# Norm of the last feed-forward sub-layer by tiles of 128 tokens, with its first blocks in two halves of tokens

## Chip, cores and metric

The kernel runs on one core of a Trainium2 chip. The metric is the device time of one execution in microseconds (us), the median of several runs. Engines are named as in the profile: PE (matrix products and transposes), PEld (its weight loads, which overlap products), DVE (vector engine), ACT (activation engine), POOL, and SP, which here issues the DMA loads of the weights.

## What is computed

Two layers of a trunk over 256 latent tokens and 256 context tokens of 1024 channels. Each layer runs a feed-forward sub-layer, a token-mixing block and another feed-forward sub-layer; the last one of the second layer runs for the latent tokens alone. The part that matters here is the end of the last mixing block and the start of the sub-layer behind it:

```
def modulated_norm(xs, gain, mod, s):
    return rms_norm(xs, gain) * (1.0 + mod_vec(mod, 3 * s + 1)) + mod_vec(mod, 3 * s)

def gated_residual(xs, y, gain, mod, s, weight):
    return xs + weight * mod_vec(mod, 3 * s + 2) * rms_norm(y, gain)

xl = gated_residual(xl, yl, norm_post[l, 1], mod_l, 1, 1.0)      # yl: output of the mixing block
a, g = jnp.split(modulated_norm(xl, g_pre, mod, 2) @ w_in_f, 2)  # 1024 -> 2 x 2816
xl = gated_residual(xl, (jax.nn.silu(a) * g) @ w_out_f, g_post, mod, 2, 0.5)
```

## The kernel before

Tokens lie in tiles of 128 (one partition each): two latent tiles, 0 and 1, and two context tiles. A product of float32 matrices is made of three matmuls (`mm3`, lines 285 to 287), with both operands split into a rounded high part and the rest (`hi`, `lo`). The weights come by DMA into two raw buffers (`wraw`), and `Ring.ahead` splits them on ACT (`whi`, L208) and DVE (`wlo`, L211) into three pairs of buffers, a number of pieces ahead of their use. Each engine takes its instructions in the order in which the program issues them, since the schedule is written out by hand; `tick` moves a clock of the program that paces side tasks and these splits.

`natural_out` ends a sub-layer: it computes the output by token tiles with 512 channels at a time (half `h` = 0, then 1). For two tiles, and in the last half, it runs all products of tile 0, then those of tile 1. After each tile come `first` (sum of squares on ACT, `z` on DVE, L501) and `update` (reciprocal root in `rstd`, and the residual stream `x` in two halves, L512), with the squares of the new `x` for the next norm (`PreNorm.square`, L400 on ACT). In tile 1's products stands `K.W.ahead(0)`, which splits the first weights of the sub-layer behind.

When both tiles are updated, the next norm runs for both together: `stats` (L425 and `rstd`, on two columns), `scale` (`xs`, L433, four instructions), `transpose` (16 transposes on PE, L292, into PSUM banks that hold the two tiles' columns side by side), and `modulate` (ACT writes `h`, L459, 256 tokens wide, DVE splits it into `hThi`, L462, and `hTlo`, L463).

`ffn` then takes 44 blocks of 128 output channels: 11 groups `c`, each with two blocks for `a` (part 0) and two for `g` (part 1). A block is 8 x 3 matmuls with the weights as the stationary operand of 128 x 128 and the tokens as the moving operand, `N` columns: 512 in the sub-layers with context, 256 in the last one. `evacuate` takes a block out of PSUM (silu on ACT, L649, product on DVE, L653, split on both). In the sub-layers with context (`nt == 4`) the first three blocks run on the latent half (256 columns) first; `ctx_norm` stands in the middle of the third one, and then the three second halves follow. In the last sub-layer (`nt == 2`) there is no such split: every block takes its 256 columns at once.

Of the kernel before, what the change touches and what calls it, by code (L numbers as in the profile page):

```python
# [14 lines left out]
P = 128  # L15
# [240 lines left out]
def tick(K, us):  # L256

    K.clock += us
    for t in list(K.tasks):
        if t.done:  # L260
            K.tasks.remove(t)
        elif t.wake <= K.clock:
            t.step(K.clock)
# [26 lines left out]
def transpose(K, out, x):  # L290
    n = x.shape[0]
    K.nc.tensor.transpose(out, x, K.ident[:n, :n])  # L292
# [10 lines left out]
def t2k(K, name="t2k"):  # L303
    return K.tp.tile([P, 512], F32, tag="t2k", name=name)
# [98 lines left out]
class PreNorm:  # L403
# [25 lines left out]
    def scale(self, st, h):  # L429
        K = self.K  # L430
        for t in range(2):
# [2 lines left out]
                                      scalar2=None, op0=OP.mult)  # L434
            self.xs[h, t] = xs

    def transpose(self, st, h, bank=aux_tile):
        K = self.K
        pts = [bank(K) for _ in range(2)]
        for b in range(4):  # L440
            for t in range(2):
                o = 256 * (b % 2) + P * t
                transpose(K, pts[b // 2][:, o:o + P], self.xs[h, t][:, P * b:P * b + P])
        self.pts[h] = pts
# [21 lines left out]
def natural_out(K, y1, lhi, llo, nk, wview, tiles, G, nxt, hold, free):  # L466
# [55 lines left out]
    for h in range(2):  # L522
        pss = {t: mm_tile(K) for t in tiles}
        nh = len(hold) if h == 1 and hold and len(tiles) > 2 else min(3 + h * len(hold), n)
        for i in range(n - nh):
            s = piece(i, h, None if h == 1 and hold else min(K.W.nsub - 1, n - 1 - i))
            for t in tiles:
                part(pss[t], s, t)
        if h == 0:
            subs = [piece(i, h, n - 1 - i) for i in range(n - nh, n)]  # L530
            for t in tiles:
                for j, s in enumerate(subs):
                    part(pss[t], s, t)
                    if t == tiles[-1]:
                        K.W.ahead(j)
                square_sum(K, pss[t], ss[:, t, 0:1])
                v.tensor_tensor(out=y1[:, t, :], in0=pss[t], in1=G[:, t // 2, 0:512], op=OP.mult)
            nc.scalar.activation(warm, K.ident[:, 0:1], AF.Sqrt)
            continue
        if nxt is not None:  # L540
            pn = nxt()
        if len(tiles) == 2:
            subs = [piece(i, h, min(K.W.nsub - 1, n - 1 - len(hold) - i)) for i in range(n - nh, n)]
            for t in tiles:
                for j, s in enumerate(subs):
                    part(pss[t], s, t)
                    if t == 1 and pn is not None and j == 1:
                        K.W.ahead(0)
                first(t)
                update([t])  # L550
            if pn is not None:
                pn.stats(0)
                for q in range(2):
                    pn.scale(0, q)
                    pn.transpose(0, q)
                K.W.ahead(1)
                for q in range(2):
                    pn.modulate(0, q)
        else:
            subs = []  # L560
            for i in range(n - nh, n):
                subs.append(piece(i, h, min(K.W.nsub - 1, n - 1 - i)))
                part(pss[0], subs[-1], 0)
            first(0)
            update([0])
            K.W.ahead(1)
            for s in subs:
                part(pss[1], s, 1)
            first(1)
            update([1])  # L570
            pn.stats(0)
            pn.scale(0, 0)
            pn.scale(0, 1)
            for s in subs:
                part(pss[2], s, 2)
            first(2)
            for i, s in enumerate(subs):
                part(pss[3], s, 3)
                if i < 2:
                    pn.transpose(0, i)  # L580
                    pn.modulate(0, i)
                if i == 0:
                    update([2])
            first(3)
            update([3])
            K.W.ahead(K.W.nsub - 1)
            pn.stats(1)
# [29 lines left out]
def ffn(K, l, s, f, pn, tiles, nxt, jobs, every=(5.0, 7.6), pools=None, prep=False):  # L617
# [8 lines left out]
    with pools.es as es:  # L626
# [5 lines left out]
        def mm_block(ps, sub, c0, c1, half_way=None):  # L632
            whi, wlo = sub
            for b in range(8):
                if b == 4 and half_way is not None:
                    half_way()
                mm3(K, ps[:, c0:c1], whi[:, b, :], wlo[:, b, :], hi[:, b, c0:c1], lo[:, b, c0:c1], b == 0, b == 7)
                if (b == 3 and c1 - c0 == 512) or b == 7:
                    tick(K, 2.6)

        early = []
        n_early = 3 if nt == 4 else 0
        sas = []
        blocks = [(c, part, n) for c in range(11) for part in range(2) for n in range(2)]

# [12 lines left out]
        for i, (c, part, n) in enumerate(blocks):  # L658
# [11 lines left out]
            if i >= n_early:  # L670
                mm_block(ps, sub, 0, N)
                evacuate(c, part, n, ps)
                continue
            mm_block(ps, sub, 0, 256, (lambda: ctx_norm(K, pn)) if i == n_early - 1 else None)
            early.append((ps, sub))
            if i == n_early - 1:
                for j, (ps, sub) in enumerate(early):
                    mm_block(ps, sub, 256, 512)
                    K.W.ahead(j)
                    evacuate(*blocks[j], ps)  # L680
        finish(K, ada)
# [1111 lines left out]
```

## Time and profile before

| | us |
|---|---|
| median of 3 runs (2197.65 to 2198.15) | 2197.89 |
| the profiled execution | 2197.24 |
| its span, first to last instruction | 2195.2 |

| engine | busy us | share of the span |
|---|---|---|
| PE | 2116.6 | 96% |
| PEld | 1710.9 | 78% |
| DVE | 1116.4 | 51% |
| ACT | 769.3 | 35% |

Times in the rows are us from the span's start, and those of a single instruction in the group views ns. A busy PE is not PE at its peak, since matmuls overlap each other by their latency: the distance from one start to the next tells the rate. The change lies between 1983 and 2010 us; the last sub-layer's first 44 blocks end at 2127.6 and the rest is its output.

### The profile page before, as it was taken

How to read it: one execution, taken by the hardware profiler on the slowest of the kernel's cores; microseconds unless marked ns; L12 is line 12 of the kernel's file. 1: busy time of each engine (PE TensorE's matmuls, PEld its weight loads, DVE VectorE, ACT ScalarE, POOL GpSimd, SP SyncE). 2: the span in 40 equal slices, each digit the busy share in tenths (PEclk: the TensorE clock that was granted, in tenths of full speed). 3: DMA queues.
4: the chain of work that ended last, by engine and by line, in shares of the span. 5: the costliest groups of instructions: out<-in, count | busy, mean ns of one | idle time of the engine just before them, and what ended most of it. 6: DMA issues, size and time to landing. Idle time of an engine off the chain costs nothing.

```text
span 2195.2 us, 28897 instructions
## 1 busy us (share of the span) xinstructions
PE 2116.6 (96%) x11691; PEld 1710.9 (78%) x11691; DVE 1116.4 (51%) x2038; ACT 769.3 (35%) x1282; POOL 315.9 (14%) x288
## 2 busy tenths in 40 slices
PE   6999999999999999999999999999999989998998
PEld 4766778888867778777777877778888878888997
DVE  4895332357544655633332258733324685756554
ACT  4213222343543333422222233322223345355443
POOL 0242000002323300000000024400000144440000
PEclk9999999999999999999999999999999999999999
DMA  9457542344312223355554335643223454444554
GB/s 312 172 206 257 185 146 91 115 139 135 109 62 87 76 79 112 121 176 189 182 183 164 106 117 187 225 148 115 92 82 127 171 168 128 128 140 139 188 186 145
DMA packets 211613, 323.11 MB, mean 147 GB/s; under 512 B 13176, under 2 KB 154104, under 8 KB 211480
## 3 DMA queue, kind: packets, MB, share of 16 engines
q1 hardware_dynamic: 196864, 287.17, 38.4%
q0 software_dynamic: 8560, 27.63, 3.9%
q10 hardware_dynamic: 6056, 6.46, 1.0%
q8 instruction: 92, 1.51, 0.3%
q14 instruction: 41, 0.34, 0.0%
HBM read 307.57 MB, written 14.71 MB: 147 GB/s over the span
## 4 chain that ended last, share of the span: by engine, by line
PE 82%; DVE 9%; issue 3%; ACT 3%; DMA 2%; POOL 1%; ACTq 0%; DVEq 0%; SPq 0%; POOLq 0%
PE mm L285 25%; PE mm L286 24%; PE mm L287 24%; PE aux L341 3%; PE aux L292 2%; DVE wlo L211 1%; DVE hTlo L463 1%; PE aux L1434 1%; DMA wraw<-in_w_ffn_in_dram 1%; ACT jk L400 1%; ACT whi L208 1%; PE aux L1559 1%; DVE hThi L462 1%; DVE at_mx L1408 1%; PE aux L1157 1%
## 5 line engine op out<-in xcount | busy, mean ns | idle before, releaser
L285 PE MATMUL mm<-hThi,whi 128*128 128x512 f32 (+1 forms) x1992 | 716.1, 360 | 10.4 <-DVE hThi L462 5.5
L287 PE MATMUL mm<-hThi,wlo 128*128 128x512 f32 (+1 forms) x1992 | 699.6, 351 | 7.3 <-DVE wlo L211 4.0
L286 PE MATMUL mm<-hTlo,whi 128*128 128x512 f32 (+1 forms) x1992 | 699.9, 351 | 1.5 <-DVE hTlo L463 0.7
L211 DVE TENSOR_TENSOR wlo<-wraw,whi 128x1024 fp32r<-128x1024 f32 (+1 forms) x295 | 362.5, 1234 | 429.6 <-ACT whi L208 428.1
L285 PEld LDWEIGHTS mm<-hThi,whi 128*128 128x128 f32 x1992 | 379.3, 190 | 120.4 <-issue 49.6
L208 ACT ACTIVATE whi<-wraw 128x1024 fp32r<-128x1024 f32 (+1 forms) x351 | 367.1, 1049 | 235.0 <-PE mm L287 173.7
L287 PEld LDWEIGHTS mm<-hThi,wlo 128*128 128x128 f32 x1992 | 379.3, 190 | 59.5 <-DVE wlo L211 5.4
L286 PEld LDWEIGHTS mm<-hTlo,whi 128*128 128x128 f32 x1992 | 379.5, 191 | 50.2 <-DVE hTlo L463 4.0
L211 POOL TENSOR_TENSOR wlo<-wraw,whi 128x1024 fp32r<-128x1024 f32 x56 | 138.0, 2471 | 239.9 <-ACT whi L208 223.1
L653 DVE TENSOR_TENSOR sa<-sa,mm 128x512 f32<-128x512 f32 (+1 forms) x88 | 54.3, 617 | 145.4 <-PE mm L287 145.4
L649 ACT ACTIVATE sa<-mm 128x512 f32<-128x512 f32 (+1 forms) x88 | 47.7, 543 | 216.1 <-PE mm L287 214.3
L286 PE MATMUL mm<-wlo,ha 128*128 128x512 f32 x308 | 120.0, 389 | 0.0
L285 PE MATMUL mm<-whi,ha 128*128 128x512 f32 x308 | 120.0, 389 | 0.0
L287 PE MATMUL mm<-whi,ha 128*128 128x512 f32 x308 | 119.8, 389 | 0.0
L655 ACT ACTIVATE ha<-sa 128x512 fp32r<-128x512 f32 (+1 forms) x44 | 25.4, 578 | 244.0 <-DVE sa L653 244.0
L655 ACT ACTIVATE hb<-sa 128x512 fp32r<-128x512 f32 (+1 forms) x44 | 25.5, 579 | 178.3 <-DVE sa L653 169.8
L285 PE MATMUL mm<-whi,hThi 128*128 128x512 f32 (+2 forms) x224 | 81.9, 366 | 5.1 <-ACT whi L208 5.1
L286 PE MATMUL mm<-wlo,hThi 128*128 128x512 f32 (+2 forms) x224 | 80.5, 359 | 2.4 <-DVE wlo L211 2.4
L388 POOL DMA_DIRECT2D gd<-ev x12 | 6.8, 574 | 513.9 <-ACT whi L208 356.7
L287 PE MATMUL mm<-whi,hTlo 128*128 128x512 f32 (+2 forms) x224 | 79.5, 355 | 0.0
L285 PE MATMUL mm<-whi,hb 128*128 128x512 f32 x188 | 73.1, 389 | 0.0
L286 PE MATMUL mm<-wlo,hb 128*128 128x512 f32 x188 | 73.1, 389 | 0.0
(441 smaller groups left out, 2859.5 us busy)
## 6 DMA issues: line engine op xcount, KB each, us to landing
wraw<-in_w_ffn_in_dram SPq DMA_DIRECT2D x88, 1024.0 KB
wraw<-in_w_in_dram SPq DMA_DIRECT2D x42, 1024.0 KB
wraw<-in_w_ffn_out_dram SPq DMA_DIRECT2D x40, 1024.0 KB
adaG<-in_w_ada_dram SPq DMA_DIRECT2D x33, 1024.0 KB
aday<-in_w_ada_dram SPq DMA_DIRECT2D x33, 1024.0 KB
wraw<-in_w_out_dram SPq DMA_DIRECT2D x7, 1024.0 KB
ha<-in_w_ada_dram SPq DMA_DIRECT2D x6, 1024.0 KB
r_tq<-tab SPq DMA_DIRECT2D x8, 768.0 KB
```

The costliest lines, as they stand in the source:

```text
L208: K.nc.scalar.activation(h3, r, AF.Copy)
L211: (self.eng or K.lo_eng).tensor_tensor(out=l3, in0=r, in1=h3.bitcast(F32), op=OP.subtract)
L285: mm(out, ahi, bhi, start=first, stop=False)
L286: mm(out, ahi, blo, start=False, stop=False)
L287: mm(out, alo, bhi, start=False, stop=last)
L292: K.nc.tensor.transpose(out, x, K.ident[:n, :n])
L341: nc.tensor.matmul(ps[o:o + 32, :], self.K.sc[:, k + i, :], w[:, i, 512 * b:512 * b + 512], start=k == 0, stop=k == 6, tile_position=(0, o))
L400: K.nc.scalar.activation(jk[:, :src.shape[-1]], src, AF.Square, scale=1.0 / 32.0, accum_out=acc)
L462: nc.vector.tensor_copy(oh, hv)
L649: nc.scalar.activation(sa[:, :N], ps[:, :N], AF.Silu)
L653: nc.vector.tensor_tensor(out=g[:, :N], in0=g[:, :N], in1=ps[:, :N], op=OP.mult)
L655: nc.scalar.activation(hh, g[:, :N], AF.Copy)
```

## The change

It replaces the norm of both tiles by two norms of one tile each, in the last mixing block only (the one place where `natural_out` has two tiles and a norm behind it). `tile_scale(t)` runs directly behind `update([t])`, inside the loop over tiles: sum, reciprocal root and the scaling of that tile's two halves. `tile_out(t, dve)` makes 8 transposes into two PSUM banks (one for each half of the channels) and modulates one tile: of four blocks of 128 x 128, three on ACT and the one in `dve` on DVE, and DVE splits 512 elements into the tile's columns of `hThi` and `hTlo`. Tile 0's `tile_out` stands behind the loop, tile 1's in the middle of the third block's first half. The last sub-layer's first three blocks get the two halves that the others have, here of 128 columns, and `tick` counts a half of 128 columns as 1.3 in place of 2.6. The number of pieces that are split ahead in these three blocks becomes 2, 1 and 0 instead of 2 each, and the splits stand behind the second halves.

```diff
+    def tile_scale(self, t):
+        K = self.K
+        rs = K.sm.tile([P, 2], F32, tag="pn_rs", name="pn_rs", bufs=2)[:, 0:1]
+        rst = K.sm.tile([P, 2], F32, tag="pn_rst", name="pn_rst", bufs=2)[:, 0:1]
+        ss = self.ss[0]
+        K.nc.vector.scalar_tensor_tensor(out=rs, in0=ss[:, t:t + 1, 0], scalar=RMS_EPS, in1=ss[:, t:t + 1, 1], op0=OP.add, op1=OP.add)
+        rstd(K, rst, rs, 1)
+        for h in range(2):
+            xs = t2k(K, "xs")
+            K.nc.vector.tensor_scalar(out=xs, in0=K.x[:, t, 512 * h:512 * h + 512], scalar1=rst, scalar2=None, op0=OP.mult)
+            self.xs[h, t] = xs
+
+    def tile_out(self, t, dve):
+        K, nc, v = self.K, self.K.nc, self.K.nc.vector
+        A, B = K.AB[self.l, self.s]
+        pts = [aux_tile(K) for _ in range(2)]
+        for h in range(2):
+            for b in range(4):
+                transpose(K, pts[h][:, P * b:P * b + P], self.xs[h, t][:, P * b:P * b + P])
+        for h in range(2):
+            h32 = t2k(K, "h32")
+            for b in range(4):
+                o, p = h32[:, P * b:P * b + P], pts[h][:, P * b:P * b + P]
+                a, c = A[:, 4 * h + b, 0:1], B[:, 4 * h + b, 0:1]
+                if b in dve:
+                    v.tensor_scalar(out=o, in0=p, scalar1=a, scalar2=c, op0=OP.mult, op1=OP.add)
+                else:
+                    nc.scalar.activation(o, p, AF.Identity, scale=a, bias=c)
+            hv = h32.rearrange("p (k c) -> p k c", k=4)
+            oh = self.hi[:, 4 * h:4 * h + 4, P * t:P * t + P]
+            v.tensor_copy(oh, hv)
+            v.tensor_tensor(out=self.lo[:, 4 * h:4 * h + 4, P * t:P * t + P], in0=hv, in1=oh.bitcast(F32), op=OP.subtract)
...
                 first(t)
                 update([t])
+                if pn is not None:
+                    pn.tile_scale(t)
             if pn is not None:
-                pn.stats(0)
-                for q in range(2):
-                    pn.scale(0, q)
-                    pn.transpose(0, q)
+                pn.tile_out(0, (3,))
                 K.W.ahead(1)
-                for q in range(2):
-                    pn.modulate(0, q)
...
-                    tick(K, 2.6)
+                    tick(K, min(2.6, (c1 - c0) / 98.0))
...
-        n_early = 3 if nt == 4 else 0
+        n_early = 3
...
-            mm_block(ps, sub, 0, 256, (lambda: ctx_norm(K, pn)) if i == n_early - 1 else None)
+            mm_block(ps, sub, 0, N // 2, (lambda: ctx_norm(K, pn) if nt == 4 else pn.tile_out(1, (3,))) if i == n_early - 1 else None)
...
-                    mm_block(ps, sub, 256, 512)
+                    mm_block(ps, sub, N // 2, N)
```

## Rows read from the trace of the kernel before

**Rows 1.** The page's first part: each engine's busy time, share and instructions

```profile
PE 2116.6 (96%) x11691; PEld 1710.9 (78%) x11691; DVE 1116.4 (51%) x2038; ACT 769.3 (35%) x1282; POOL 315.9 (14%) x288
```

**Rows 2.** Stretches: length, busy us of PE, PEld, DVE, ACT, POOL, PEclk, DMA share, GB/s

```profile
1988.70:1996.25 7.55, 0.00 (x0) 0.00 (x1) 5.30 (x16) 3.83 (x10) 1.05 (x2) 0.65 0.11 30
1996.25:1999.76 3.51, 3.51 (x16) 3.30 (x17) 3.35 (x7) 2.17 (x5) 0.00 (x0) 0.50 0.77 241
1999.76:2003.70 3.94, 3.85 (x26) 3.65 (x25) 3.84 (x8) 3.81 (x6) 0.00 (x0) 0.82 0.80 266
2003.70:2009.50 5.80, 5.80 (x50) 5.80 (x49) 2.87 (x3) 2.66 (x4) 0.00 (x0) 1.00 0.31 98
2009.50:2127.60 118.10, 118.10 (x987) 118.10 (x986) 65.88 (x82) 54.32 (x81) 0.00 (x0) 1.00 0.55 183
```

**Rows 3.** Waits of PE from 1983 to 2010: who waited for whom, us, times, longest

```profile
PE aux L292 <- DVE xs L433: 7.6, 1, 7.6
```

**Rows 4.** DVE's timeline around the norm: start, us, instruction, idle before and releaser

```profile
1985.88 0.75 DVE L512 SCALAR_TENSOR_TENSOR x<-z,po_rst,x 128x512 f32<-128x512 f32 x1
...
1989.19 1.23 DVE L211 TENSOR_TENSOR wlo<-wraw,whi 128x1024 fp32r<-128x1024 f32 x1 [1.89 <-ACT whi L208]
1990.33 0.68 DVE L501 TENSOR_TENSOR z<-mm,G 128x512 f32<-128x512 f32 x1
...
1992.14 0.75 DVE L512 SCALAR_TENSOR_TENSOR x<-z,po_rst,x 128x512 f32<-128x512 f32 x1
...
1994.49 0.16 DVE L425 SCALAR_TENSOR_TENSOR pn_rs<-pn_ss 128x2 f32<-128x2 f32 x1 [0.94 <-ACT jk L400]
...
1995.71 1.68 DVE L433 TENSOR_SCALAR xs<-x,pn_rst 128x512 f32<-128x512 f32 x4
...
1998.64 0.43 DVE L462 CAST hThi<-h 128x512 fp32r<-128x512 f32 x1
1999.10 0.69 DVE L463 TENSOR_TENSOR hTlo<-h,hThi 128x512 fp32r<-128x512 f32 x1
```

**Rows 5.** ACT's timeline over the same stretch

```profile
1988.12 1.04 ACT L208 ACTIVATE whi<-wraw 128x1024 fp32r<-128x1024 f32 x1
1989.07 0.57 ACT L400 ACTIVATE jk<-mm 128x512 f32<-128x512 f32 x1
...
1997.59 3.75 ACT L459 ACTIVATE h<-aux,mB,mA 128x256 f32<-128x256 f32 x8 [1.75 <-PE aux L292]
```

**Rows 6.** PE's timeline: the first product of the sub-layer and the first of block 3

```profile
1999.76 0.56 PE L285 MATMUL mm<-hThi,whi 128*128 128x256 f32 x1
...
2009.50 0.28 PE L285 MATMUL mm<-hThi,whi 128*128 128x256 f32 x1
```

**Rows 7.** PE's timeline: 16 transposes of an earlier norm at full clock

```profile
43.91 1.91 PE L292 MATMUL aux<-ident,xs 128*128 128x128 f32 x16
```

**Rows 8.** Groups by form (busy us, mean ns, idle), and one timeline row of L1362

```profile
L1417 ACT ACTIVATE at_p<-aux,at_nm 128x512 f32<-128x512 f32 x32 | 21.7, 683 | 62.8 <-DVE at_nm L1410 28.4 <-DVE at_nm L1414 24.4 <-DVE at_es L1420 9.9
L1417 ACT ACTIVATE at_p<-aux,at_nm 128x256 f32<-128x256 f32 x16 | 7.4, 470 | 21.6 <-DVE at_nm L1410 11.4 <-DVE at_nm L1414 10.1
L1567 DVE CAST br<-aux 128x128 fp32r<-128x128 f32 x12 | 3.4, 287 | 6.3 <-PE aux L1434 6.3
L1362 PE MATMUL aux<-zg,wT 128*128 128x128 f32 x8 | 1.3, 287 | 0.0
1807.52 0.61 PE L1362 MATMUL aux<-zg,wT 128*128 128x128 f32 x4
```

**Rows 9.** Groups by form: products of 512 and 256 columns, loads of 128 and 32

```profile
L286 PE MATMUL mm<-hTlo,whi 128*128 128x512 f32 x1240 | 483.8, 390 | 0.0
L286 PE MATMUL mm<-hTlo,whi 128*128 128x256 f32 x752 | 216.1, 287 | 1.5 <-DVE hTlo L463 0.7
L285 PEld LDWEIGHTS mm<-hThi,whi 128*128 128x128 f32 x1992 | 379.3, 190 | 120.4 <-issue 49.6 <-ACT sa L649 15.1 <-ACT whi L208 4.0
L341 PEld LDWEIGHTS aux<-adaG,sc 128*32 128x32 f32 x256 | 5.4, 108 | 8.2 <-issue 7.2
```

## The prediction

> **What bounds the kernel now.** I read the page first: the matrix engine (PE) is busy 96% of the span [rows 1], so only stretches in which it isn't doing wanted products can be won. The table by stretches then shows the place of the change: after the last product of the mixing block PE does nothing for 7.55 us (1988.70 to 1996.25), spends 3.51 us on the 16 transposes of the norm at a granted clock of 0.50, and from 2009.50 to 2127.60 is busy 118.10 of 118.10 us [rows 2]. The waits say what the 7.55 us are: the first transpose waits for `xs`, the scaled tokens [rows 3]. The DVE and ACT timelines show the serial chain in between (residual, squares, reciprocal root, scale, transpose, modulate, split) [rows 4, 5]. The last stretch is the key to the sum: its products run without any wait, 41 blocks of 24, so 118.10 / 984 = 0.12 us each, and any shift of the first of them, at 2009.50 [rows 6], moves the end by the same amount. I therefore work out when the first product of block 3 (the fourth block of the sub-layer, counted from 0) starts after the change, and compare it with 2009.50. Before, the three blocks ahead of it take 2009.50 - 1999.76 = 9.74 us, of which 72 x 0.12 = 8.64 are products at full clock.
>
> **Tile 0's norm comes earlier.** The chain of tile 1 takes 1994.49 - 1992.14 = 2.35 us from its first residual update to the sum of squares, and 1995.71 - 1994.49 = 1.22 from there to `xs` [rows 4]. Applied to tile 0, whose first update is at 1985.88 [rows 4], the sum stands at 1988.23, the root on ACT at 1988.42, `xs` at 1989.45 and, two halves of 0.40 each (four take 1.68), done at 1990.25. PE is free by then, and its 8 transposes run behind tile 1's products, at full clock (it has stood for under 1 us): (1.91 - 0.27) / 15 = 0.11 each, 0.9 us in all [rows 7], until about 1990.9. They cost nothing, being covered by tile 1's chain, which lasts to 1997.
>
> **Tile 1's norm comes later.** The work put in front of it: on ACT the weight conversion of the first block (1988.12) and the square of tile 1 (1989.07) [rows 5] now stand behind tile 0's root, so they move to 1988.54 and 1989.49. On DVE the conversion's second half (1989.19) stands behind tile 0's two scalings and starts at 1990.25, and tile 1's `z`, which follows it, moves from 1990.33 to 1991.39: 1.06 us. The rest of its chain keeps its lengths: first update 1993.20, sum 1995.55, `xs` 1996.77, done at 1997.57.
>
> **The modulation of tile 0 is queued behind that.** `tile_out(0)` stands after the loop, so on ACT it follows tile 1's root and on DVE tile 1's scalings, and each engine takes its instructions in order. ACT: 8 of 256 columns take 3.75 us, one lasting some 0.57 [rows 5], so they start 0.45 apart; 128 columns fewer at (683 - 470) ns / 256 = 0.83 ns a column [rows 8] give about 0.35 (estimate), and the three of the first half are done by 1997.1. DVE: the fourth block of 128 columns (some 0.24 apart; 0.29 for one [rows 8]) from 1997.57, `hi` from 1997.81 and `lo` at 0.46 behind it, ready at 1998.97 (0.43 and 0.69 [rows 4]). PE's first product goes at about 1998.3, the second, which needs `lo`, at 1998.98. The front of the stage gains 0.8 us, not the 7.55: the wait for `xs` is replaced by a wait for `hi` and `lo`. That is the same wait seen from PE, a little shorter, and what is queued behind it is the whole feed-forward block.
>
> **Narrow products.** The three blocks are now done as 72 products with 128 moving columns and 72 more with the other 128. Each still loads the same 128 x 128 weights: 144 loads in place of 72. Streaming costs (390 - 287) ns / 256 columns = 0.40 ns a column [rows 9], which would make a product 0.067 us if only the stream counted (0.12 less 128 x 0.417). But the load is not free: 128 columns take 190 ns and 32 take 108 [rows 9], so 0.85 ns a column, twice the stream, and 128 columns hold the loader about 0.11 us. At 256 moving columns (0.107 us) the two are level; at 128 the loader should set the pace. No row has this kind of product under 256 columns. The nearest is L1362: 128 moving columns behind a full load of 128 columns, four in 0.61 us and 287 ns for one, (0.61 - 0.29) / 3 = 0.11 each [rows 8]; it is two passes of plain f32, so it shows that the loader keeps 0.11 and not that it can do less. Bounds: 0.067 (stream alone) and 0.22 (a whole f32 product of this shape is two such passes). I take 0.12, the spacing at 256, since the loader's 0.11 is nearest to it. So half the width saves nothing, and the second halves are extra.
>
> **Clock.** PE stands from 1990.9 to 1998.3, as it does now from 1988.70 to 1996.25 with the clock falling to 0.50 [rows 2]. Now the 16 transposes and some products run at half clock; it rises about 4.9 us after PE's first work (0.50 throughout the stretch from 1996.25, and a mean of 0.82 over the next 3.94 us puts the rise 1.4 us into it, near 2001.2 [rows 2]). After the change there are only products there: 4.9 us from 1998.3 means 4.2 us from the second product at 0.213, 20 products that lose 0.093 each, 1.8 us (1.0 to 2.7 if it rises 2 us sooner or later).
>
> **Tile 1 in mid-block.** 8 transposes stand in PE's stream: 8 x 0.11 = 0.9. From their start ACT begins after 0.65, `hi` is ready after 2.3 and `lo` after 3.0 (the DVE and ACT steps above); PE has 0.9 + 12 x 0.12 = 2.3 us of work, so it waits 0.6 on `lo`; the second half of the channels is ready in time. On ACT and DVE only two weight conversions stand ahead, done by 2003.
>
> **Edits with no price.** No DMA is moved on any queue. The ticks: 2.6 for 256 columns as before, 1.3 for 128, and no ada task runs here. The conversion of block 3's weights moves behind block 0's second half, but 48 products (5.8 us) stand between it and its use, against 2.3 us for the conversion; without that cover it would cost the 2.3. DMA share is 0.55 in the last stretch [rows 2], the loads get more time and not less. The table load for silu on ACT falls in the same cover. The first feed-forward blocks elsewhere keep their halves of 256.
>
> **Sum.** 1998.98 + 71 x 0.12 (8.52) + 1.8 + 0.9 + 0.6 + 72 x 0.12 (8.64) = 2019.4, against 2009.50: 9.9 us later, with no wait behind to absorb it [rows 2]. The profiled execution took 2197.24 us for a span of 2195.2, and the median of the runs shown is 0.65 above it: 2207.1 for a like execution, 2207.8 as a median. Own range 2205 to 2210.5 (0.11 to 0.125 a product, the clock as above).
>
> **Rivals.**
> *The loader keeps up (not slower).* If loads hide behind short streams, a narrow product costs 0.067. At half clock 39 fit into the 4.2 us, 32 more take 2.1, transposes 0.9: 2006.2. Now PE outruns tile 1's modulation: `lo` comes at 2007.5 and its second half at 2008.8, and 60 products take 4.0: 2012.8, 3.3 us later, 2201.1. For: the products of 256 columns can't tell a loader of 0.11 from a faster one. Against: the slope of the loads. It decides below 0.08 us a product, where the loss falls under 4.4 us (0.2%, about what a measurement of this kernel can tell from no change).
> The Trainium skill, TensorE: Matmul & The Clock Gate, section Back-to-back issue gap, gives a sustained 81 ns per product at 128 columns in a stream of loads and products. By it the sum would be 4.4 us up, 2202.2, on the edge between this rival and a loss; no row here has such a product, and the slope of the f32 loads speaks for more.
> *Narrow products fall to the f32 rate (slower still).* At 0.22 us a product: 4.2 us at half clock hold 9, then 62 x 0.22 and 72 x 0.22, 0.9 for transposes, no wait on `lo`: 25 us later, 2222.8. For: no row of this type is under 256 columns. Against: nothing in rows at 256 to 512 hints at a second rate.
> *The order isn't what I read:* tile 0's modulation runs ahead of tile 1's norm. Then products start near 1993 and tile 1 is ready before it is needed, but 144 x 0.12 + 1.5 still end at about 2012: 2200.3. Against: DVE's order before follows the program [rows 4].
> A gain would need 144 products, 0.9 us of transposes and the cold start within 10.5 us, under 0.055 a product; the stream alone forbids it.
>
> **Chances.** Forecast 0.62, loader keeps up 0.15, f32 rate 0.18, other order 0.05. Slower by over 0.2%: the forecast, the f32 rate and a bit of the first rival, 0.82; within: 0.16; faster: 0.02. The range takes in both bounds of the narrow product: 2201 to 2223.
>
> **What would show it.** In the profile of the changed kernel: 8 transposes near 1990 at full clock; the first product with `hThi` near 1998.3 behind DVE `hi`, not `xs`; spacing of the 128-column products 0.12 (0.067 and 0.22 are the rivals); 8 transposes inside the third block, a wait of some 0.6 on `lo`; block 3's first 256-column product near 2019.4, and from there to the end the same length as before. I am wrong if the spacing is another, or if tile 0's modulation is found ahead of tile 1's scaling.

## The result, and the profile after

The changed kernel takes 2221.09 us (median of 5 runs, 2211.44 to 2223.47) against 2197.89 for the kernel before: ratio 1.0091 with the 95% interval 1.0061 to 1.0120, so some 20 us slower by the ratio and 23 by the medians. The profiled execution took 2223.21 us, with a span of 2221.2. Its frame lies 2.06 us later than the earlier one already ahead of the change (the last product of the mixing block ends at 1990.76, before at 1988.70 [rows 2]), so times below are compared by their distance from that point.

The first part of the page of the changed kernel (busy time, share and instructions of each engine):

```profile
PE 2139.9 (96%) x11763; PEld 1733.5 (78%) x11763; DVE 1119.4 (50%) x2047; ACT 770.7 (35%) x1287; POOL 315.8 (14%) x288
```

Its waits of PE from 1985 to 2035 us (who waited for whom, us in total, times, longest):

```profile
PE mm L285 <- DVE hThi L469: 7.5, 1, 7.5
PE aux L292 <- DVE xs L447: 1.3, 1, 1.3
PE mm L286 <- DVE hTlo L470: 0.2, 1, 0.2
```

PE is busy 23.3 us longer than in [rows 1], with 72 products more. The wait of 7.6 us for `xs` [rows 3] is now one of 7.5 for `hThi`: it has only moved from ahead of the transposes to behind them. PE's timeline in the changed kernel (start, us, instruction, and idle before with its releaser):

```profile
1990.37 0.39 PE L287 MATMUL mm<-whh,mlo 128*128 128x512 f32 x1
1992.05 1.09 PE L292 MATMUL aux<-ident,xs 128*128 128x128 f32 x8 [1.30 <-DVE xs L447]
2000.61 0.44 PE L285 MATMUL mm<-hThi,whi 128*128 128x128 f32 x1 [7.47 <-DVE hThi L469]
2001.25 0.47 PE L286 MATMUL mm<-hTlo,whi 128*128 128x128 f32 x1 [0.19 <-DVE hTlo L470]
2001.52 0.41 PE L287 MATMUL mm<-hThi,wlo 128*128 128x128 f32 x1
2001.74 0.41 PE L285 MATMUL mm<-hThi,whi 128*128 128x128 f32 x1
...
2013.90 1.93 PE L292 MATMUL aux<-ident,xs 128*128 128x128 f32 x8
...
2033.44 0.52 PE L285 MATMUL mm<-hThi,whi 128*128 128x256 f32 x1
```

DVE's timeline of the same kernel, ahead of the first product:

```profile
1998.81 0.88 DVE L447 TENSOR_SCALAR xs<-x,pn_rst 128x512 f32<-128x512 f32 x2
1999.61 0.40 DVE L464 TENSOR_SCALAR h<-aux,mA,mB 128x128 f32<-128x128 f32 x1
```

The order is the one forecast: tile 0's transposes behind tile 1's products, tile 0's modulation behind tile 1's scaling, tile 1's transposes inside the third block. But the narrow products follow each other every 0.213 us (2001.52, 2001.74), and block 3 begins at 2033.44, which is 42.68 us behind the mixing block's end; before it was 2009.50 - 1988.70 = 20.80 [rows 2, 6]. The table by stretches of the changed kernel (columns as in [rows 2]) tells why:

```profile
1990.70:1994.30 3.60, 1.15 (x9) 0.86 (x8) 3.32 (x9) 1.59 (x4) 0.00 (x0) 1.00 0.00 0
1994.30:2000.61 6.31, 0.00 (x0) 0.03 (x1) 4.59 (x16) 4.39 (x13) 1.05 (x2) 0.50 0.33 94
2000.61:2013.90 13.29, 13.09 (x61) 12.91 (x61) 4.29 (x6) 1.37 (x2) 0.00 (x0) 0.50 0.34 115
2013.90:2033.44 19.54, 19.54 (x94) 19.54 (x94) 5.42 (x8) 6.26 (x11) 0.00 (x0) 0.50 0.17 55
2033.44:2038.70 5.26, 5.26 (x26) 5.26 (x27) 1.98 (x3) 1.47 (x2) 0.00 (x0) 0.50 0.33 101
2038.70:2150.00 111.30, 111.30 (x929) 111.30 (x929) 62.10 (x77) 52.75 (x78) 0.00 (x0) 1.00 0.53 171
```

The granted clock (PEclk) is 0.50 from 1994.30 to 2038.70, thus 1.2 of 2.4 GHz for 44 us. It stays there through all 144 narrow products, though PE has no gap in them but the first ones, and comes back 5.2 us after the products of 256 columns have begun. Before, it rose 1.4 us into the products (near 2001.2), and the low stretch had lasted 10.2 us in all.

So the loss of the profiled execution adds up: 21.88 us more up to block 3; 2.34 more in the 41 blocks behind it, which begin with 5.26 us at half clock; 0.28 less in the output; 2.06 from the frame: 26.0, which is 2221.2 - 2195.2. Not each execution had the clock low that long. The five times fall into two groups, two near 2211.5 and three at 2221 to 2223.5, and the mean granted clock falls with them (0.984 and 0.985 against 0.979, 0.979 and 0.978).

### The profile page after: what moved, and what is told of

Same layout as the page of the kernel before. It is cut to its first block, busy times and chain, and to the rows that moved or that the text cites. A ratio compares the mean times of both kernels' runs of the same rounds, so it can differ in the third digit from the quotient of the medians.

```text
span 2221.2 us, 29061 instructions
## 1 busy us (share of the span) xinstructions
PE 2139.9 (96%) x11763; PEld 1733.5 (78%) x11763; DVE 1119.4 (50%) x2047; ACT 770.7 (35%) x1287; POOL 315.8 (14%) x288
## 4 chain that ended last, share of the span: by engine, by line
PE 82%; DVE 10%; ACT 3%; issue 3%; DMA 2%; POOL 1%; ACTq 0%; DVEq 0%; SPq 0%; POOLq 0%
PE mm L285 25%; PE mm L287 24%; PE mm L286 24%; PE aux L341 3%; PE aux L292 2%; DVE wlo L211 1%; DVE hTlo L498 1%; PE aux L1466 1%; ACT jk L400 1%; DMA wraw<-in_w_ffn_in_dram 1%; PE aux L1591 1%; ACT whi L208 1%; DVE hThi L497 1%; DVE at_mx L1440 1%; PE aux L1189 1%
## 5 line engine op out<-in xcount | busy, mean ns | idle before, releaser
L285 PE MATMUL mm<-hThi,whi 128*128 128x512 f32 (+2 forms) x2016 | 730.8, 362 | 16.6 <-DVE hThi L469 7.5
L287 PE MATMUL mm<-hThi,wlo 128*128 128x512 f32 (+2 forms) x2016 | 714.6, 354 | 7.8 <-DVE wlo L211 4.5
L286 PE MATMUL mm<-hTlo,whi 128*128 128x512 f32 (+2 forms) x2016 | 714.9, 355 | 1.9 <-DVE hTlo L498 1.0
L285 PEld LDWEIGHTS mm<-hThi,whi 128*128 128x128 f32 x2016 | 392.3, 195 | 126.6 <-issue 49.4
L287 PEld LDWEIGHTS mm<-hThi,wlo 128*128 128x128 f32 x2016 | 392.4, 195 | 60.2 <-DVE wlo L211 6.0
L286 PEld LDWEIGHTS mm<-hTlo,whi 128*128 128x128 f32 x2016 | 392.4, 195 | 50.9 <-DVE hTlo L498 3.8
```

The lines of the kernel that those rows point to most:

```text
L285: mm(out, ahi, bhi, start=first, stop=False)
L286: mm(out, ahi, blo, start=False, stop=False)
L287: mm(out, alo, bhi, start=False, stop=last)
```

## The experiments

For each profile the table gives the distance from the end of the mixing block's last product to the first product of block 3, and its difference to the 20.80 us of before. That leaves out the frame. Each ratio is to executions of the kernel before from the same session; their medians were 2197.89, 2198.03, 2198.87 and 2198.41 us.

| kernel | median us (range) | ratio to before, interval | distance, difference |
|---|---|---|---|
| changed kernel | 2221.09 (2211.44 to 2223.47) | 1.0091, 1.0061 to 1.0120 | 42.68, +21.88 |
| norm_by_tile | 2202.23 (2200.03 to 2207.64) | 1.0017, 1.0009 to 1.0026 | 24.68, +3.88 |
| halves_only | 2208.05 (2203.10 to 2223.10) | 1.0049, 1.0032 to 1.0067 | 28.34, +7.54 |
| after_filled | 2218.50 (2210.48 to 2221.25) | 1.0083, 1.0066 to 1.0100 | 35.48, +14.68 |
| before_filled | 2198.30 (2196.28 to 2202.99) | 1.0003, 0.9995 to 1.0012 | 20.58, -0.22 |
| quarters | 2252.11 (2251.03 to 2253.20) | 1.0240, 1.0223 to 1.0258 | 73.36, +52.56 |
| short_loads | 2209.77 (2208.14 to 2211.39) | 1.0048, 1.0030 to 1.0066 | 29.76, +8.96 |
| second_pass_whole | 2213.42 (2211.15 to 2219.43) | 1.0071, 1.0057 to 1.0086 | 35.78, +14.98 |
| filled_tile1_earlier | 2207.95 (2206.00 to 2209.00) | 1.0039, 1.0027 to 1.0051 | 27.55, +6.75 |
| halves_filled | 2221.97 (2219.50 to 2223.71) | 1.0103, 1.0088 to 1.0118 | 41.07, +20.27 |
| tile1_earlier | 2215.86 (2206.81 to 2221.68) | 1.0067, 1.0045 to 1.0090 | 42.68, +21.88 |

### The two halves of the change, each alone

**The norm by tile with whole blocks** (norm_by_tile; edited from the changed kernel):

```diff
-        n_early = 3
+        n_early = 3 if nt == 4 else 0
...
                 pn.tile_out(0, (3,))
+                pn.tile_out(1, (3,))
```

> The norm by tiles as in the change, but every block takes its 256 columns at once, and tile 1's transposes and modulation stand ahead of block 0. Theory 1 (narrow products are paced by the weight load, and under them the granted clock stays at its lower level): no narrow products, so only the front differs; tile 1's low part is ready near 2001.5 instead of 1999.8, clock back up within 5 us as in the kernel before: 0 to 3 us over the kernel before. Rival (the loss comes from the norm by tiles, its order on ACT and DVE and the longer wait): 10 us or more of the 23 us stay.

Measured: 2202.23 us. PE's waits from 1983 to 2010 us in this kernel:

```profile
PE aux L292 <- DVE xs L447: 7.5, 2, 6.2
PE mm L285 <- DVE hThi L469: 2.3, 1, 2.3
```

Splitting the norm alone costs about 4 us, a little more than the 0 to 3 that theory 1 expected and far from the rival's 10. PE now waits 7.5 + 2.3 us, against 7.6 before [rows 3], since tile 1 still has its whole modulation to go when its transposes are done. The first product starts 2000.47 - 1987.61 = 12.86 us behind the mixing block, against 1999.76 - 1988.70 = 11.06. The rest of the 3.88 is a longer stretch of products at half clock.

**The halves with the norm of both tiles as before** (halves_only; edited from the kernel before, `tick` as in the change):

```diff
-        n_early = 3 if nt == 4 else 0
+        n_early = 3
...
-            mm_block(ps, sub, 0, 256, (lambda: ctx_norm(K, pn)) if i == n_early - 1 else None)
+            mm_block(ps, sub, 0, N // 2, (lambda: ctx_norm(K, pn)) if nt == 4 and i == n_early - 1 else None)
...
-                    mm_block(ps, sub, 256, 512)
+                    mm_block(ps, sub, N // 2, N)
```

> The norm for both tiles together as in the kernel before, but the first three blocks in halves of 128 columns, with nothing between the halves. Theory 1: narrow products at 0.213 us from start to start as long as the clock is at 0.50, and it stays there through most of the 144: 15 to 23 us over the kernel before. If the clock rises some 5 us after PE's first work as it did before, 144 x 0.12 us: about 8 us over. Rival (norm by tiles): under 3 us. Rival (f32 rate, 0.22 us at full clock and twice that at half): over 24 us.

Measured: 2208.05 us over 12 runs, ten of them from 2203.10 to 2211.73 and two at 2220.14 and 2223.10. The stretches of its profile:

```profile
1994.30:2004.50 10.20, 5.10 (x24) 4.88 (x24) 8.28 (x22) 6.53 (x16) 1.05 (x2) 0.50 0.46 153
2004.50:2020.20 15.70, 15.52 (x138) 15.38 (x138) 5.19 (x6) 4.93 (x6) 0.00 (x0) 1.00 0.22 71
```

Here the clock rises at 2004.50, 5.1 us behind the start of the 16 transposes at 1999.40, as in the kernel before (2001.2 against 1996.25), and 138 products fit into 15.70 us: 0.11 us each, half the width for nearly the time of 0.12 that the double width takes. That is the forecast's main term. The time is 10.0 us over its session's kernel before (2198.03), near the 8 that were expected if the clock rises as before; that it stays low through most of the 144 products, 15 to 23 us, was a miss in ten of the twelve. In these profiles the two halves of the change by themselves come to 3.88 + 7.54 = 11.4 us. The changed kernel lost 21.88 in its own; the rest goes with the clock, which came back early in these two profiles and not in that one.

### What sets the pace of a narrow product

**Two quarters in place of a half** (quarters): 64 moving columns, twice as many loads.

```diff
-            mm_block(ps, sub, 0, N // 2, (lambda: ctx_norm(K, pn) if nt == 4 else pn.tile_out(1, (3,))) if i == n_early - 1 else None)
+            mid = (lambda: ctx_norm(K, pn) if nt == 4 else pn.tile_out(1, (3,))) if i == n_early - 1 else None
+            if nt == 4:
+                mm_block(ps, sub, 0, N // 2, mid)
+            else:
+                mm_block(ps, sub, 0, 64)
+                mm_block(ps, sub, 64, 128, mid)
...
-                    mm_block(ps, sub, N // 2, N)
+                    if nt == 4:
+                        mm_block(ps, sub, N // 2, N)
+                    else:
+                        mm_block(ps, sub, 128, 192)
+                        mm_block(ps, sub, 192, 256)
```

> The changed kernel with each half of the first three blocks cut into two pieces of 64 moving columns: 288 products instead of 144, the same columns in all, the same 128 x 128 weights loaded twice as often. Theory 1 (the weight load sets the pace): the distance between products stays at about 0.11 us at full clock and 0.213 at half, so the stage grows by 16 to 31 us over the changed kernel. Rival (narrow products stream two cycles a column): the distance halves with the columns, to about 0.055 and 0.107, and the stage keeps its time within 5 us.

**Loads of 64 columns** (short_loads): the moving width stays 128; the other 64 output channels of the three blocks are left out (set to zero).

```diff
+            m = P if nt == 4 else 64
+            if nt == 2:
+                nc.vector.memset(ps, 0.0)
...
-                mm3(K, ps[:, c0:c1], whi[:, b, :], wlo[:, b, :], hi[:, b, c0:c1], lo[:, b, c0:c1], b == 0, b == 7)
+                mm3(K, ps[:m, c0:c1], whi[:, b, :m], wlo[:, b, :m], hi[:, b, c0:c1], lo[:, b, c0:c1], b == 0, b == 7)
```

> The changed kernel with the first three blocks loading only 64 of the 128 weight columns, 128 moving columns as in the change: the other 64 channels of these blocks are left out (set to zero on DVE). Theory 1 (the weight load sets the pace): half the load is 0.053 us, so at full clock products follow each other every 0.067 us, the stream with its 0.013, and every 0.107 to 0.12 at half clock, in place of 0.111 and 0.213. Rival (two cycles a moving column): 0.111 and 0.213 as before.

Measured: 2252.11 and 2209.77 us. PE's timeline in quarters, at half clock:

```profile
1999.08 0.40 PE L285 MATMUL mm<-hThi,whi 128*128 128x64 f32 x1
1999.29 0.40 PE L286 MATMUL mm<-hTlo,whi 128*128 128x64 f32 x1
1999.50 0.40 PE L287 MATMUL mm<-hThi,wlo 128*128 128x64 f32 x1
```

PE's timeline in short_loads, at half clock up to 2011.9 and at full clock behind it:

```profile
2009.12 0.34 PE L285 MATMUL mm<-hThi,whi 128*64 128x128 f32 x1 [12.57 <-DVE mm L708]
...
2009.47 0.31 PE L285 MATMUL mm<-hThi,whi 128*64 128x128 f32 x1
2009.58 0.31 PE L286 MATMUL mm<-hTlo,whi 128*64 128x128 f32 x1
...
2011.97 0.22 PE L285 MATMUL mm<-hThi,whi 128*64 128x128 f32 x1
2012.03 0.22 PE L286 MATMUL mm<-hTlo,whi 128*64 128x128 f32 x1
```

With half of the moving columns the distance stays 0.213 us; with half of the weight columns it falls to 0.107, and to 0.06 at full clock (0.067 was expected). So the weight load sets the pace of a product of 128 columns, not the stream and not a slower arithmetic rate. The total of short_loads says nothing beside this, since zeroing the banks held back the first product by 12.57 us.

The same trace bears on the clock. It rose 2.8 us behind the first of these products (2009.12 to 2011.9). At 2018.7 it fell, and at 2022.1 it rose again, still under products of 128 columns, as their spacing in short_loads shows:

```profile
2021.80 0.31 PE L285 MATMUL mm<-hThi,whi 128*64 128x128 f32 x1
2021.90 0.31 PE L286 MATMUL mm<-hTlo,whi 128*64 128x128 f32 x1
...
2022.19 0.22 PE L286 MATMUL mm<-hTlo,whi 128*64 128x128 f32 x1
2022.25 0.22 PE L287 MATMUL mm<-hThi,wlo 128*64 128x128 f32 x1
```

So a narrow moving side by itself does not keep the clock low. Whether the halved load made the difference to the changed kernel is not shown by this one profile.

### What becomes of the clock

**Filled gap, with the change** (after_filled) **and without** (before_filled): 31 or 32 products of 512 columns into an unused bank, at the place where PE would stand.

```diff
+    def fill(n):
+        ps = aux_tile(K)
+        w = subs[-1][1][0]
+        for _ in range(n):
+            nc.tensor.matmul(ps, lhi(0)[:, 0:P], w[:, 0, :], start=True, stop=True)
...
                 pn.tile_out(0, (3,))
+                fill(31)
```

In the kernel before, with the same `fill`:

```diff
             if pn is not None:
+                fill(32)
                 pn.stats(0)
```

> The changed kernel with 31 extra products of 512 columns into a PSUM bank that nobody reads, behind tile 0's transposes, while PE waits for tile 0's modulation: they take about 7 us and leave the output as it is. Theory 1: the clock is at its full level when the narrow products start and their spacing there is 0.12 us; if narrow products also hold it there, block 3 starts some 8 us later than in the kernel before (+8 us in all); if the clock falls under them, the spacing goes to 0.213 and the loss lies between 8 and 23 us. Rival (f32 rate): 0.22 us at full clock, +24 us.

> The kernel before with 32 extra products of 512 columns into a PSUM bank that nobody reads, between tile 1's last product and the norm's transposes. It prices the clock's fall in the kernel before. The clock stays at its full level and the 16 transposes take 1.9 us instead of 3.5; since DVE's splits set the pace up to about 2003 us, both theories expect little: 0 to 2 us faster. If the rest is unchanged in that measure, a cold start alone does not make the 23 us of the changed kernel.

Measured: 2218.50 and 2198.30 us. In before_filled the clock is full throughout and nothing is won: DVE's splits set the pace of the first products, so the cold start of the kernel before costs it nothing that can be measured. In after_filled the narrow products begin at full clock, 0.111 us apart, and then lose it. Its stretches:

```profile
1990.93:2008.89 17.96, 16.78 (x114) 14.84 (x113) 11.05 (x27) 7.96 (x20) 1.05 (x2) 1.00 0.35 118
2008.89:2010.30 1.41, 1.01 (x7) 0.87 (x8) 1.38 (x3) 0.09 (x1) 0.00 (x0) 0.99 0.00 0
2010.30:2024.27 13.97, 13.97 (x68) 13.97 (x67) 3.19 (x4) 4.05 (x5) 0.00 (x0) 0.50 0.24 76
```

and its first two products of tile 1:

```profile
2008.89 0.33 PE L285 MATMUL mm<-hThi,whi 128*128 128x128 f32 x1 [0.43 <-DVE hThi L469]
2009.62 0.33 PE L286 MATMUL mm<-hTlo,whi 128*128 128x128 f32 x1 [0.40 <-DVE hTlo L470]
```

At full speed PE outruns tile 1's modulation, waits 0.43 and 0.40 us for it, and the clock falls right behind these waits, at 2010.3, and stays low for 17 us. That the waits are its cause is not shown by this: ahead of its first two narrow products, at 1998.66 and 1999.30, PE waited 0.41 and 0.34 us, and the clock stayed full for another 11 us.

**All 44 blocks in halves** (all_halves, and all_halves_again for two more executions; edited from the kernel before, `tick` as in the change): is a narrow product enough to lose the clock?

```diff
             if i >= n_early:
-                mm_block(ps, sub, 0, N)
+                if nt == 4:
+                    mm_block(ps, sub, 0, N)
+                else:
+                    mm_block(ps, sub, 0, N // 2)
+                    mm_block(ps, sub, N // 2, N)
```

> The kernel before with all 44 blocks of the last sub-layer in halves of 128 columns one after the other, 2112 narrow products in a row without any wait. Theory 1: 0.111 us each at full clock, so at least 107 us more than before, and the granted clock doesn't stay up under them: long parts of the stretch at 0.50, where they take 0.213, up to 320 us more. Rival (the low clock comes from the idle gap ahead and is a matter of a few us): 0.50 only in the first 10 us, then full level, 107 us more.

> All 44 blocks in halves of 128, once more, for more executions. If unbroken narrow products at full clock hold it in every execution: 2306 to 2309 us each, as the first (2307.47). If the level is not sure under them: executions longer by up to 2112 x 0.1 = some 200 us, with stretches at 0.50 and 0.213 us between products.

Measured: 2307.47, then 2306.69 and 2308.53 us (these two: ratio 1.0493, 1.0472 to 1.0514). The first profile's stretches:

```profile
1992.10:2002.30 10.20, 4.85 (x23) 4.64 (x23) 8.25 (x23) 6.31 (x15) 1.05 (x2) 0.50 0.47 143
2002.30:2130.00 127.70, 127.52 (x1140) 127.32 (x1140) 40.45 (x50) 33.45 (x49) 0.00 (x0) 1.00 0.29 97
```

It isn't: with no wait but one of 0.18 us, narrow products hold the full clock, in both profiles to the end of the 44 blocks. Theory 1 missed here and its rival came out. The sum fits too: 2112 x 0.111 - 1056 x 0.12 = 108 us, and 109 were measured.

**Second pass over all 256 columns** (second_pass_whole): the second halves computed at the old width, so that more is streamed with the same loads.

```diff
-                    mm_block(ps, sub, N // 2, N)
+                    mm_block(ps, sub, N // 2 if nt == 4 else 0, N)
```

> The changed kernel, but the second pass over the first three blocks takes all 256 columns again instead of the last 128: more columns for the same result, the number of products and loads the same. Theory 1 (narrow products keep the clock low, wide ones raise it): the first pass runs at 0.213 us a product as in the changed kernel, in the second the clock rises within some 5 us, and then 256 columns take 0.12 us where 128 took 0.213: about 5 us faster than the changed kernel at its slow times, +18 us over the kernel before. Rival (the level has nothing to do with the width): the same time as the changed kernel or up to 2 us more.

Measured: 2213.42 us. It does more work than the changed kernel and is not slower; the two intervals overlap, so that it is faster isn't shown. Its stretches:

```profile
2000.00:2012.59 12.59, 12.59 (x59) 12.59 (x60) 3.60 (x5) 0.66 (x1) 0.00 (x0) 0.50 0.32 107
2012.59:2016.33 3.74, 3.74 (x22) 3.74 (x22) 1.37 (x3) 2.20 (x6) 0.00 (x0) 0.57 0.00 0
2016.33:2030.00 13.67, 13.67 (x114) 13.56 (x114) 6.70 (x11) 6.31 (x9) 0.00 (x0) 1.00 0.30 99
```

The clock rises at 2015.8, in the narrow products behind the 8 transposes of tile 1 and just before the first wide product. So wide products aren't what it had to wait for in this execution; up to here its order is that of the changed kernel, whose profile shows no rise at that place.

**Tile 1's norm one block earlier, with the filler and without** (filled_tile1_earlier, tile1_earlier), so that nothing has to be waited for in mid-stream; **and the halves alone with the filler** (halves_filled):

```diff
-            mm_block(ps, sub, 0, N // 2, (lambda: ctx_norm(K, pn) if nt == 4 else pn.tile_out(1, (3,))) if i == n_early - 1 else None)
+            mm_block(ps, sub, 0, N // 2, (lambda: ctx_norm(K, pn) if nt == 4 else pn.tile_out(1, (3,))) if i == (n_early - 1 if nt == 4 else n_early - 2) else None)
```

> The filled kernel with tile 1's tile_out moved from the middle of the third block's first half to the middle of the second block's, so that its modulation has about 5 us of products beside it and PE has nothing to wait for. Theory (the two waits of 0.43 and 0.40 us on tile 1's modulation are what let the clock fall at 2010.3 in the filled kernel): full clock through all 144 narrow products, 0.111 us each, block 3 at 1999.3 + 71 x 0.111 + 0.9 + 72 x 0.111 = 2016.1, 6.6 us later than before: 2204.6 us against 2198.0 (2203 to 2207), and no time near 2220. Rival (narrow products let the clock fall with or without a wait): a stretch at 0.50 with a spacing of 0.213 stays, and the time with it, 2211 to 2221.

> The changed kernel with tile 1's tile_out in the middle of the second block's first half, no filler: PE is cold at the first product as in the changed kernel. If what decides is only that PE starts the narrow products at 0.50 and that they can't be counted on to raise it, the place of the 8 transposes changes little: 2211 to 2223 us with executions at both ends, as in the changed kernel. If the 8 transposes raise the clock when nothing has to be waited for around them, it rises near 2009 in each execution: 24 + 12 products at 0.213 and the rest at 0.111, some 4 us above a full-clock run, 2209 (2207 to 2212).

> The kernel with the halves only (norm of both tiles as before), and 32 products of 512 columns into an unused bank behind the last product of the mixing block, so that PE is busy until the transposes. Both theories of the clock expect full clock at the start of the narrow products; no wait lies within them. Theory (only waits let it fall): full clock to the end, 144 x 0.111 in place of 72 x 0.120, 7.3 us more: 2205.4 us (2203 to 2207) in each execution, without the two of twelve at 2220 and 2223 that the halves alone showed. Rival (narrow products let it fall by themselves now and then): some executions at 2210 to 2223 stay.

Measured: 2207.95, 2215.86 and 2221.97 us. The first has no fall and, in five executions, no time near 2220, as the theory of the waits expected, though its median lies 0.95 us above that theory's range. Its stretches:

```profile
1993.48:2001.22 7.74, 7.31 (x35) 5.75 (x33) 5.91 (x19) 4.49 (x13) 1.05 (x2) 1.00 0.28 75
2001.22:2018.89 17.67, 17.33 (x152) 17.10 (x153) 9.71 (x14) 7.54 (x13) 0.00 (x0) 1.00 0.35 118
```

The second spreads like the changed kernel: with a cold start the place of the transposes settles nothing. The third was a miss for the theory, and for the rival too, which expected some executions at 2210 to 2223: all four lie at 2219.50 to 2223.71. The filler makes the halves 12 us slower by the ratios, 14 by the medians. Its first products on PE's timeline:

```profile
2000.04 0.33 PE L285 MATMUL mm<-hThi,whi 128*128 128x128 f32 x1 [0.41 <-DVE hThi L462]
2000.77 0.33 PE L286 MATMUL mm<-hTlo,whi 128*128 128x128 f32 x1 [0.40 <-DVE hTlo L463]
...
2001.83 0.33 PE L286 MATMUL mm<-hTlo,whi 128*128 128x128 f32 x1 [0.18 <-DVE hTlo L463]
```

The stretches of halves_filled:

```profile
1989.67:2002.20 12.53, 11.18 (x59) 8.88 (x58) 10.01 (x25) 7.84 (x19) 1.05 (x2) 1.00 0.32 114
2002.20:2030.90 28.70, 28.70 (x136) 28.64 (x136) 5.25 (x6) 4.92 (x6) 0.00 (x0) 0.50 0.18 61
```

I had written that no wait lies within its narrow products. That was wrong: at full clock PE runs into DVE's splits and waits 0.41, 0.40 and 0.18 us there, and the clock falls at 2002.20 for 30.7 us. Before_filled is the same kernel with 256 columns: the same filler, waits for the same splits (0.41 and 0.34 us on the first two products), and no fall, as these two products and a stretch of before_filled show:

```profile
2002.69 0.39 PE L285 MATMUL mm<-hThi,whi 128*128 128x256 f32 x1 [0.41 <-DVE hThi L462]
2003.42 0.38 PE L286 MATMUL mm<-hTlo,whi 128*128 128x256 f32 x1 [0.34 <-DVE hTlo L463]
...
2000.04:2014.00 13.96, 12.89 (x96) 11.65 (x97) 10.39 (x16) 8.92 (x15) 0.00 (x0) 1.00 0.58 198
```

So waits and narrow products together stand at each fall inside this stage (after_filled, halves_filled, and short_loads, where it falls at 2018.7 among waits of 1.00, 0.45 and 0.45 us); wide products with such waits (before_filled), or narrow ones with no more than a wait of 0.18 us (all_halves, halves_only from its rise on), kept the full clock in these profiles. It is no law: filled_tile1_earlier has such waits on its first two narrow products and kept the clock in its profile, and its five times agree within 3 us:

```profile
2001.22 0.30 PE L285 MATMUL mm<-hThi,whi 128*128 128x128 f32 x1 [0.43 <-DVE hThi L469]
2001.85 0.33 PE L286 MATMUL mm<-hTlo,whi 128*128 128x128 f32 x1 [0.34 <-DVE hTlo L470]
```

No version of the change here beats the kernel before. Its best form with both halves, 2207.95 us, is 0.39% slower, and each of the two halves costs by itself.

## Why the prediction was right, and which step failed

**Direction: right. Mechanism: right in part. The time: luck.** The wait of 7.6 us was not removed but moved [rows 3], and 144 narrow products cost more than 72 wide ones. With the clock full that makes 6.75 of the 21.88 us (filled_tile1_earlier, with tile 1's norm one block earlier); the other 15 or so are the low clock, for which the forecast had 1.8. The time is 13 us above the forecast's 2207.8 and outside its own range of 2205 to 2210.5. It lies inside 2201 to 2223 only because that range reaches up to the price of the f32 rate, which is not what happened. By the prediction's own sign (wrong if the spacing is another) it failed in the changed kernel: 0.213 us and not 0.12.

**Front: right.** From the end of the mixing block to the first product the forecast had 1998.3 - 1988.70 = 9.6 us, measured 2000.61 - 1990.76 = 9.85; to the second 10.28, measured 10.49. The 0.2 us are DVE's block of 128 columns: 0.40 us and not some 0.24 to 0.29 by the cast of [rows 8]. The gain of 0.8 us that the prediction names sets its second product against the first of before. Like against like, the first product was forecast 1.5 us earlier and came 1.2 earlier, from 11.06 to 9.85.

**Narrow product: right.** Taken 0.12 at full clock, measured 0.111 (filled_tile1_earlier, halves_only), and the loader is the reason, as the slope of the loads said [rows 9] and quarters and short_loads show. The rival in which the loader keeps up (0.067) is out.
The Trainium skill, TensorE: Matmul & The Clock Gate, section Back-to-back issue gap, gives a sustained 81 ns per product at 128 columns in such a stream; the narrow products here took no less than 0.111 us with a full load. The same page's section LDWEIGHTS (loading the stationary operand) gives the columns divided by 1.2 in ns; an estimate from it is 107 ns for 128. The traces come close at full clock (0.111 us) and show twice that at half clock (0.213). The 0.06 us with loads of 64 columns is no test of it, since the stream of 128 columns is about as long there (128 x 0.40 ns = 0.05 us by [rows 9]).

**The clock: the step that failed.** The forecast let the clock rise 4.9 us after PE's first work, as in the rows of before [rows 2], and put 1.8 us on it. But there PE's work was 16 transposes and products of 256 columns. In the profiled execution of the changed kernel it stayed at 0.50 for the whole stage of narrow products. From the second product to block 3 the forecast has 20.4 us, and 2033.44 - 2001.25 = 32.2 were measured: 143 x 0.213 = 30.5 in place of 143 x 0.12 + 1.8 = 19.0 (11.5 more), 1.7 in place of 0.9 for the transposes and the steps beside them at half clock (0.8 more), and no wait on tile 1 in place of 0.6, since PE was now slower than the modulation (at full clock, in after_filled, it waited 0.43 and 0.40 us there). With the 2.3 us more behind block 3's start this makes the clock about 14 us too cheap. Where the clock held, the other terms come out: in filled_tile1_earlier block 3 starts 27.55 us behind the mixing block, and the forecast's 2019.4 - 1988.70 = 30.7, less 1.8 for the clock and 143 x 0.009 for the products, is 27.6 (with a wait of 0.6 that this kernel does not have). That its median, 2207.95 us, falls on the forecast's 2207.8 is chance: its frame lies 2.64 us later than that of before (1991.34 against 1988.70).

**The rival with the nearest total is wrong.** An f32 rate of 0.22 us gave 2222.8 us, near the 2221.09 measured (the terms of that rival add up to 24.1 us and not 25, so to some 2222). But 0.213 is the load at half clock; at full clock the same instruction takes 0.111. A total that fits does not prove its mechanism; the spacing beside the granted clock does.

**Edits with no price: right.** In the changed kernel PE had no other wait between 1985 and 2035 us than the three shown, and filled_tile1_earlier had none at full clock behind its second product (17.33 of 17.67 us busy, with the wait of 0.34), so the conversions behind the second halves were covered.

**What stays open.** What decides, from one execution to the next, whether the clock rises under narrow products, and so the cause of the larger part of the loss: the changed kernel, tile1_earlier and halves_only show, by their times, both outcomes with one program. The two levels differ by 0.213 - 0.111 = 0.102 us a product, at most some 15 us over 144, which is enough for the spread of 12; that the two executions of the changed kernel near 2211.5 had an earlier rise rests on their mean clock (0.984 and 0.985), as none of them was profiled. Each of the other kernels has one profile too (all_halves has two), so what went ahead of a rise or a fall is read from single executions.

## What to carry to other kernels

Halving the moving side of a product below the width at which stream and weight load are level (here 256 columns) doubles the loads and saves nothing: price it by the load, and test that by halving each side alone. Don't price the clock by when it rose under other work: a term of 1.8 us was 14 us short. Work the sum out at either level of the clock, since one program showed both. A filler that kept PE busy won nothing where another engine set the pace of the first products (before_filled), and the kernel was slower with it where PE then ran into waits between narrow products (halves_filled).

## What the runs showed of the hardware that was not expected

- Narrow products without a gap ran at a granted clock of 0.50 for 32.8 us in the changed kernel (with tile 1's 8 transposes among them) and for over 60 us in quarters (2000 to 2061.5), and at 1.00 for the 127.70 us of the stretch shown of all_halves. The same stream of 128-column products ran at either level. With loads of 64 columns the clock rose 2.8 us behind the first such product (short_loads).
- Brief waits of 0.4 us among narrow products went ahead of a fall of the clock from its full level (after_filled, halves_filled), while such waits among products of 256 columns did not (before_filled), nor did those on the first narrow products of after_filled and filled_tile1_earlier.
The Trainium skill, TensorE: Matmul & The Clock Gate, section A second HAM failure mode: psum-queue depth-cycling, tells of short idle spells between groups of products of 512 columns, frequent enough that the clock goes back and forth. The falls here agree with it in so far as brief waits went ahead of them. But here the waits were two or three, not a steady pattern, and wide products with them kept the clock (256 columns, before_filled).
